# Attention heads taken in pairs whose products alternate between halves of the tensor engine

## The chip, the cores and the metric

The kernel runs on one core of a Trainium2 chip. The metric is the device time of one execution in microseconds, the median of several runs. TensorE (PE in the views, with PEld for its weight loads) does the matrix products, VectorE (DVE) and ScalarE (ACT) the elementwise work, GpSimd (POOL) a little of it, and SyncE (SP) issues the DMAs.

## The reference, cut to what matters

Two decoder layers on 256 tokens of width 1024, in float32. The change lies in the token mixer, which has three branches: a state-space branch (SSM) and two attentions of 8 heads of 64 features. Both attentions of a layer are, for each head,

```
s = q k^T (+ c_q - c_k for the forgetting attention)     # 256 x 256, causal
p = softmax(s)
y = p v                                                   # 256 x 64
```

where `c` is the cumulative log forget gate of the head. The SSM needs `B u` for 512 states at a time, for 256 tokens. Each layer then has a cross-attention and a feed-forward part (dense in layer 0, 8 experts in layer 1).

## The kernel before

The large products are the main work: weights stream in from HBM, ScalarE makes the short-mantissa part of each tile of [128, 1024] (L222, `split`), VectorE the rest (L229), and TensorE multiplies in three single passes (L244 to L246). One unit of main work is one such tile: 12 matmuls of 512 columns (`gemm_xs`) or 24 of 256 columns (`gemm_ws`). After each unit `tick` lets the side generators take a step: `ssm_steps` and `heads` write their instructions between the units. The order on each engine is the one in which the program stands, as a scheduler of the language then leaves it. TensorE runs in that order.

`heads` is called twice in a layer: for the forgetting attention (tiles `fqk`, `forget=True`) beside the projections of the dilated attention, and for the dilated attention (tiles `dqk`) beside the gates and the branch products. It takes one head at a step, in three stages: `weights(h)` (scores into bank `sc`, L860, softmax on VectorE and ScalarE, L868 to L875), two steps later `turn` (three transposes of `p` into bank `pt`, L882, copied by ScalarE to `pts`, L884), one step later `values` (two products into bank `py`, L894 and L896).

A product of float32 operands runs as two instructions (the views show x2 for one product of L860); the main work's float32r products are one each. The tile shape of a product says which part of the 128 x 128 array it uses: main work and transposes 128*128; scores 64*128, since a head has 64 features, and heads 0 and 1 of a pair lie on the lower and the upper 64 rows; values 128*64, the two heads of a pair on the lower and the upper 64 columns; the forget products (L863) 32*128, as the factors `fq` and `fk` have 32 rows (four blocks of eight heads; `fqh` is `fq` with the other heads' rows at zero, made by GpSimd, L856); the SSM input products (`bu`, L729) 64*128; the SSM outputs (L714) 128*32.

The products' banks come from two rotating pools, three in `mm` for the main work and five in `aux` for `sc`, `pt`, `py`, `bu` and others. `p`, `pts` and `fqh` share a pool of eight buffers.

Of the kernel before, what the change touches and what calls it, by code (L numbers as in the profile page):

```python
# [51 lines left out]
class Trunk:  # L52
    """The decoder trunk on one core.

    Products of float32 matrices run as three single-pass products of parts: each operand is
    split exactly into a part with a short mantissa and the rest (float32r tiles)."""
# [46 lines left out]
    # ---------------------------------------------------------------- pools and constants  # L103
# [37 lines left out]
    # ---------------------------------------------------------------- weight stream  # L141
# [197 lines left out]
    # ---------------------------------------------------------------- constants  # L339
    def make_constants(self):  # L340
        nc, c = self.nc, self.const
        # Columns: queries 0-127 against keys 0-127, then queries 128-255 against keys 0-255.
# [7 lines left out]
        # tri[t, q] = 1 where t <= q  # L350
# [8 lines left out]
        # Rows of the forget bias's factors, in blocks of eight heads: one column per block, the last minus  # L359
        # the first.  # L360
# [7 lines left out]
        # For the left and the right factor: weights of the two parts of c, and a constant.  # L368
# [5 lines left out]
        # fmask[p, h] = 1 where p % 8 == h  # L374
        fi = c.tile([32, 2, 8], I32, name="fi")
        nc.gpsimd.iota(fi[:, 0], pattern=[[-1, 8]], base=16, channel_multiplier=1)
        nc.vector.tensor_single_scalar(fi[:, 1], fi[:, 0], 7, op=ALU.bitwise_and)
        self.fmask = c.tile([32, 8], F32, name="fmask")
# [9 lines left out]
        # Channels of even and odd groups of 16.  # L388
# [6 lines left out]
        # The first and the second 64 partitions.  # L395
# [5 lines left out]
        # Keys that the three dilated patterns share count once for each: log of the count.  # L401
# [16 lines left out]
    def sincos(self, ang, sin, cosm1, w):  # L418
        """sin and cos - 1 of ang (which is overwritten), by halved angles; w: a tile as large."""
# [73 lines left out]
    def statistics(self, src):  # L493
        """[mean, 1 / standard deviation] of the tokens of src (two halves of 512 columns)."""
# [56 lines left out]
        # exp(a) - 1: by tanh where |a| < 1.  # L551
# [14 lines left out]
        # lambda_bar - 1 and its quotient by lambda.  # L566
# [17 lines left out]
        # lambda_bar; its square's radius and phase.  # L584
# [8 lines left out]
    def double_angle(self, dst, ph):  # L593
        """dst: (cos, sin) of twice the angle of ph."""
# [7 lines left out]
    def complex_mul(self, dst, src, p, w, conj=False):  # L602
        """dst = src * p (or its conjugate). dst, src: [128, 2, a, b]; p: [128, 2, a]; w: [128, 2, 1024]."""
# [27 lines left out]
        # b_bar and lambda_bar b_bar, in blocks of two groups, transposed to [(lag, 32 channels), 128 states]  # L631
        # for two pieces at a time.
# [19 lines left out]
        # C and minus its imaginary part in the same blocks; then times the conjugate of lambda_bar.  # L652
# [25 lines left out]
        # exp(i 2 theta c) for c < 128 by doubling.  # L678
# [20 lines left out]
    def ssm_steps(self, l):  # L699
        """The states' recurrence as a real one in a turning frame, 512 states at a time; leaves y before  # L700
        the GELU in uy[:, 1], then its GELU."""
# [19 lines left out]
        for k in range(4):  # L721
# [3 lines left out]
            for q in range(4):  # L725
                r = slice(64 * (q % 2), 64 * (q % 2) + 64)
                bu = self.bank(self.aux, "bu")[:, :2 * P].rearrange("p (j c) -> p j c", j=2)
                for j in range(2):
                    nc.tensor.matmul(bu[:, j], bt[r, j, 2 * k + q // 2], us[r, q // 2, k], start=True, stop=True,  # L729
                                     tile_position=(r.start, 0))  # L730
                nc.vector.tensor_mul(v[:, 0, :, q], bu, cc[:, :, q])
                nc.vector.tensor_mul(v[:, 1, :, q], bu, ss[:, :, q])
                if q == 1:
# [23 lines left out]
        # Twice the GELU of y, and the parts of the GELU.  # L757
# [15 lines left out]
    def few_weights(self, src):  # L773
        """Parts of a [1024, 8] matrix, its columns over and over to fill the tensor engine's."""
# [9 lines left out]
    def few_outputs(self, wp):  # L784
        """x @ w for a matrix of 8 columns, as [8, tokens]."""
# [7 lines left out]
    def forget_bias(self, l):  # L793
        """Factors of c_q - c_k over all heads, c the cumulative log forget gates: rows of parts."""
# [12 lines left out]
        # log sigmoid(z) = min(z, 0) - log1p(exp(-|z|))  # L807
# [24 lines left out]
        fq = self.sm([32, S], "fq", bufs=1)  # L832
        fk = self.sm([32, S], "fk", F32R, bufs=1)
        for i, dst in ((0, fq), (3, fk)):
# [4 lines left out]
        self.forget = (fq, fk)  # L839
        yield  # L840

    def heads(self, qk, v, yt, bias, forget=False):
        """Softmax attention of 8 heads, in three stages, two steps and one step apart. qk: [128 (2 heads x 64), 2, 4, 256],
        v: [128 tokens, 2, 512], yt: parts [128, 2, 4, 256] of the transposed result."""
        nc = self.nc
        spans = ((0, slice(0, P)), (1, slice(P, 384)))
        st, py = {}, {}

        def weights(h):
            hp, j = h // 2, h % 2  # L850
            r = slice(64 * j, 64 * j + 64)
            q, k = qk[r, 0, hp], qk[r, 1, hp]
            ps = self.bank(self.aux, "sc")
# [10 lines left out]
            p = self.work([P, 512], "p")  # L864
            mx = self.sm([P, 6], "mx", bufs=4)
            # Minus the scores and minus their maximum.
            for t, cs in spans:
                nc.vector.tensor_tensor_reduce(p[:, cs], ps[:, cs], bias[:, cs], -1.0, 3e38, op0=ALU.add,  # L868
# [586 lines left out]
```

## Time and profile before

| | |
|---|---|
| median of 3 runs (lowest, highest) | 1417.94 us (1417.54, 1419.36) |
| profiled execution: span from its first to its last instruction | 1416.7 us |
| TensorE matmuls busy | 1387.9 us (98%) |
| VectorE busy | 1078.7 us (76%) |
| ScalarE busy | 814.2 us (57%) |
| GpSimd busy | 58.0 us (4%) |

The profiled execution has its span as its own time; the runs' median is 1.2 us above it. Matmuls overlap in the records: one of 512 columns is shown with 0.39 us, and the next starts 0.23 us after it. So a busy share of TensorE hides short stops, and what an instruction costs is read from the distance of the starts. The first product of a new tile shape is recorded from the start of its weight load.

In layer 0 the forgetting attention lies at 100.4 to 157.8 us and the dilated one at 164.0 to 217.5 us; in layer 1 they lie at 678.3 to 737.6 us and 743.9 to 797.6 us.

### The profile page before, as it was taken

Reading aid. Unit: us, or ns where it says so; the run is one execution under the profiler, and the core shown is the slowest. Engines: PE = TensorE matmul, PEld = TensorE weight load, DVE = VectorE, ACT = ScalarE, POOL = GpSimd, SP = SyncE. Lnnn points to the kernel's source line nnn. Section 1 sums busy time; section 2 is a strip of 40 time slices with the busy share of each in tenths; the row PEclk is TensorE's granted clock in tenths of the full one; section 3 lists DMA queues with packets and bytes.
Section 4 is the critical chain, followed back from the end, with each engine's and each line's share of the span. In section 5 each row is a group of like instructions: output and inputs, shape, how many; then the busy total and the mean of one; then the engine's idle time right before and its main releaser. Section 6 shows DMA issues by size and latency. Waiting matters only on the chain. (4 is left out here: it accounts for less than half of the span.)

```text
span 1416.7 us, 22446 instructions
## 1 busy us (share of the span) xinstructions
PE 1387.9 (98%) x8918; PEld 1224.6 (86%) x8918; DVE 1078.7 (76%) x1721; ACT 814.2 (57%) x1170; POOL 58.0 (4%) x79
## 2 busy tenths in 40 slices
PE   7999999999999999999999999998999999999996
PEld 6996889989899999889678999897888888888884
DVE  6797768678585687567666666867899888989887
ACT  4656554445444544434556545443687777877774
POOL 1111000000000000010100000004000000000000
PEclk9999999999999999999999999998999999999998
DMA  9451327755764346635333756563599999999980
GB/s 313 106 179 60 115 88 234 249 179 179 260 191 130 112 129 235 226 118 166 102 100 114 247 183 219 180 253 112 220 364 330 348 349 327 354 346 324 358 326 32
DMA packets 187409, 299.48 MB, mean 211 GB/s; under 512 B 19288, under 2 KB 113568, under 8 KB 187296
## 3 DMA queue, kind: packets, MB, share of 16 engines
q1 hardware_dynamic: 187296, 297.97, 61.4%
q8 instruction: 72, 1.18, 0.3%
q14 instruction: 41, 0.34, 0.1%
HBM read 295.85 MB, written 1.05 MB: 210 GB/s over the span
## 5 line engine op out<-in xcount | busy, mean ns | idle before, releaser
L229 DVE TENSOR_TENSOR split<-raw,split 128x1024 fp32r<-128x1024 f32 (+1 forms) x555 | 648.9, 1191 | 195.8 <-ACT split L222 188.8
L222 ACT CAST split<-raw 128x1024 fp32r<-128x1024 f32 (+1 forms) x558 | 563.8, 1026 | 296.8 <-PE bank L246 96.6
L244 PE MATMUL bank<-xth,split 128*128 128x256 f32 x1056 | 302.2, 286 | 0.0
L245 PE MATMUL bank<-xtl,split 128*128 128x256 f32 x1056 | 298.9, 283 | 0.0
L246 PE MATMUL bank<-xth,split 128*128 128x256 f32 x1056 | 298.8, 283 | 0.0
L244 PEld LDWEIGHTS bank<-xth,split 128*128 128x128 f32 x1056 | 202.3, 192 | 5.9 <-issue 5.1
L245 PEld LDWEIGHTS bank<-xtl,split 128*128 128x128 f32 x1056 | 202.4, 192 | 0.4
L246 PEld LDWEIGHTS bank<-xth,split 128*128 128x128 f32 x1056 | 202.4, 192 | 0.3 <-issue 0.2
L244 PE MATMUL gu<-split,xgh 128*128 128x512 f32 (+1 forms) x384 | 144.4, 376 | 0.0
L245 PE MATMUL gu<-split,xgh 128*128 128x512 f32 (+1 forms) x384 | 143.0, 372 | 0.1
L246 PE MATMUL gu<-split,xgl 128*128 128x512 f32 (+1 forms) x384 | 142.8, 372 | 0.0
L245 PEld LDWEIGHTS gu<-split,xgh 128*128 128x128 f32 x384 | 72.2, 188 | 11.3 <-DVE split L229 1.4
L246 PEld LDWEIGHTS gu<-split,xgl 128*128 128x128 f32 x384 | 72.1, 188 | 10.2
L244 PEld LDWEIGHTS gu<-split,xgh 128*128 128x128 f32 x384 | 72.2, 188 | 10.0
L245 PE MATMUL yd<-split,hth 128*128 128x512 f32 x176 | 69.1, 393 | 0.0
L246 PE MATMUL yd<-split,htl 128*128 128x512 f32 x176 | 68.8, 391 | 0.0
L244 PE MATMUL yd<-split,hth 128*128 128x512 f32 x176 | 62.3, 392 | 0.0
L244 PE MATMUL bank<-split,xth 128*128 128x512 f32 x128 | 54.2, 423 | 5.1 <-ACT xth L234 5.1
L246 PE MATMUL bank<-split,xtl 128*128 128x512 f32 x128 | 51.7, 405 | 0.3 <-DVE xtl L237 0.3
L245 PE MATMUL bank<-split,xth 128*128 128x512 f32 x128 | 51.7, 405 | 0.0
L503 POOL TENSOR_TENSOR lnrs<-lnrs,neghalf 128x1 f32<-128x1 f32 x12 | 11.1, 922 | 976.7 <-DVE lnrs L502 976.7
L871 ACT ACTIVATE p<-p,mx 128x128 f32<-128x128 f32 x64 | 28.7, 449 | 27.0 <-DVE mx L868 26.9
(418 smaller groups left out, 2476.9 us busy)
## 6 DMA issues: line engine op xcount, KB each, us to landing
raw<-in_w_in_dram SPq DMA_DIRECT2D x52, 1024.0 KB, 5.3
raw<-in_moe_w_down_dram SPq DMA_DIRECT2D x40, 1024.0 KB, 6.7
raw<-in_moe_w_gate_dram SPq DMA_DIRECT2D x32, 1024.0 KB, 7.3
raw<-in_moe_w_up_dram SPq DMA_DIRECT2D x32, 1024.0 KB, 7.3
raw<-in_w_branch_dram SPq DMA_DIRECT2D x12, 1024.0 KB, 5.2
raw<-in_moe_w_gate_dram SPq DMA_DIRECT2D x16, 768.0 KB, 7.1
raw<-in_moe_w_up_dram SPq DMA_DIRECT2D x16, 768.0 KB, 6.2
raw<-in_ffn_w_gate_dram SPq DMA_DIRECT2D x11, 1024.0 KB, 5.2
```

The costliest lines, as they stand in the source:

```text
L222: self.nc.scalar.copy(t[:, 0], raw)
L229: self.nc.vector.tensor_sub(t[:, 1], raw, t[:, 0].bitcast(F32))
L244: mm(ps, lh, rh, start=first, stop=False)
L245: mm(ps, lh, rl, start=False, stop=False)
L246: mm(ps, ll, rh, start=False, stop=last)
L503: nc.gpsimd.tensor_tensor(rs[:, 1:2], rs[:, 0:1], self.neghalf, op=ALU.pow)
L871: nc.scalar.activation(p[:, cs], p[:, cs], AF.Exp, bias=mx[:, t:t + 1], scale=-1.0, accum_out=mx[:, 2 + t:3 + t])
```

## The change

Heads are taken in pairs. `weights(hp)` writes the scores of both heads, alternating between the row halves, into two banks, then the forget products of both, then both softmaxes; it runs at even steps. `values(hp)` writes the products of both heads, alternating between the column halves, at even steps, one step after the transposes of the pair's second head. `turn` stays one head at a step. The forget factors become tiles of 128 rows, filled with zeros once at the start, of which the first 32 are written; the masked factor `fqh` of 128 rows is made by ScalarE, no longer by GpSimd, and the forget products use the whole array. In `ssm_steps` two groups of input products take their banks together, and their products alternate between the row halves. Comments were also removed, which moves line numbers: L860, L863, L882 and L894/L896 become L864, L868, L890 and L899, L729 becomes L734.

```diff
 make_constants:
+        self.fq = c.tile([P, S], F32, name="fq")
+        self.fk = c.tile([P, S], F32R, name="fk")
+        nc.gpsimd.memset(self.fq, 0.0)
+        nc.gpsimd.memset(self.fk.bitcast(F32), 0.0)
...
 ssm_steps:
-            for q in range(4):
-                r = slice(64 * (q % 2), 64 * (q % 2) + 64)
-                bu = self.bank(self.aux, "bu")[:, :2 * P].rearrange("p (j c) -> p j c", j=2)
+            for i in range(2):
+                bus = [self.bank(self.aux, "bu")[:, :2 * P].rearrange("p (j c) -> p j c", j=2) for _ in range(2)]
                 for j in range(2):
-                    nc.tensor.matmul(bu[:, j], bt[r, j, 2 * k + q // 2], us[r, q // 2, k], start=True, stop=True,
-                                     tile_position=(r.start, 0))
+                    for bu, r in zip(bus, (slice(0, 64), slice(64, P))):
+                        nc.tensor.matmul(bu[:, j], bt[r, j, 2 * k + i], us[r, i, k], start=True, stop=True,
+                                         tile_position=(r.start, 0))
...
 heads:
-        def weights(h):
...
-            if forget:
-                fq = self.work([32, S], "fqh", F32R)
-                nc.gpsimd.tensor_scalar(fq, self.forget[0], self.fmask[:, h:h + 1], None, op0=ALU.mult)
-            for t, cs in spans:
-                ts = slice(t * P, t * P + P)
-                nk = P * (t + 1)
-                nc.tensor.matmul(ps[:, cs], q[:, ts], k[:, :nk], start=True, stop=not forget,
-                                 tile_position=(r.start, 0))
-                if forget:
-                    nc.tensor.matmul(ps[:, cs], fq[:, ts], self.forget[1][:, :nk], start=False, stop=True)
+        def weights(hp):
+            pair = [self.bank(self.aux, "sc") for _ in range(2)]
+            fqs = []
+            if forget:
+                for j in range(2):
+                    h = 2 * hp + j
+                    fqs.append(self.work([P, S], "fqh", F32R))
+                    nc.scalar.activation(fqs[j], self.fq, AF.Copy, scale=self.fmask[:, h:h + 1])
+            for t, cs in spans:
+                for ps, r in zip(pair, halves):
+                    nc.tensor.matmul(ps[:, cs], qk[r, 0, hp, t * P:t * P + P], qk[r, 1, hp, :P * (t + 1)],
+                                     start=t == 0 or not forget, stop=not forget, tile_position=(r.start, 0))
+            for ps, fq in zip(pair, fqs):
+                for t, cs in spans:
+                    nc.tensor.matmul(ps[:, cs], fq[:, t * P:t * P + P], self.fk[:, :P * (t + 1)],
+                                     start=False, stop=t == 1)
+            for j, ps in enumerate(pair):
...
-        def values(h, pts):
...
+        def values(hp):
+            o = self.bank(self.aux, "py")
+            for kt, (q, c) in enumerate(((slice(0, S), slice(0, S)), (slice(P, S), slice(S, 384)))):
+                for j, r in enumerate(halves):
+                    h = 2 * hp + j
+                    nc.tensor.matmul(o[r, q], v[:, kt, h * HD:(h + 1) * HD], st[h][:, c], start=kt == 0,
+                                     stop=kt == 1, tile_position=(0, r.start))
...
         for i in range(NH + 3):
-            if i >= 3:
-                values(i - 3, st.pop(i - 3))
+            if i % 2 == 0:
+                if i >= 4:
+                    values(i // 2 - 2)
+                if i < NH:
+                    weights(i // 2)
             if 2 <= i < NH + 2:
-                st[i - 2] = turn(st[i - 2])
-            if i < NH:
-                st[i] = weights(i)
+                turn(i - 2)
             yield
```

TensorE at a step of the forgetting attention of layer 0, before (main work is L244 to L246, `py` are values, `pt` transposes, `sc` scores and forget products):

```order
L894 MATMUL py<-pts,vv 64x256
L896 MATMUL py<-pts,vv 64x128
L882 MATMUL pt<-ident,p 128x128 x3
L860 MATMUL sc<-fqk 128x128
L245 MATMUL bank<-split,xth 128x512
L246 MATMUL bank<-split,xtl 128x512
L863 MATMUL sc<-fk,fqh 128x128
L860 MATMUL sc<-fqk 128x256
L863 MATMUL sc<-fk,fqh 128x256
```

This is one head; the tile shapes change with nearly every row. TensorE at an even step of the same stage, after:

```order
L734 MATMUL bu<-us,ssmb 128x128 x4
L899 MATMUL py<-pts,vv 64x256 x2
L899 MATMUL py<-pts,vv 64x128 x2
L864 MATMUL sc<-fqk 128x128 x2
L864 MATMUL sc<-fqk 128x256 x2
L868 MATMUL sc<-fk,fqh 128x128
L868 MATMUL sc<-fk,fqh 128x256
L890 MATMUL pt<-ident,p 128x128 x3
```

These are two heads; the forget products (a 128x128 and a 128x256 for each head) and the transposes have the shape of the main work, and the odd step has the transposes of one head alone. TensorE in the dilated attention of layer 0, one head before:

```order
L894 MATMUL py<-pts,vv 64x256
L896 MATMUL py<-pts,vv 64x128
L882 MATMUL pt<-ident,p 128x128 x3
L860 MATMUL sc<-dqk 128x128
L860 MATMUL sc<-dqk 128x256
L244 MATMUL bank<-xth,split 128x256
```

The same for two heads after:

```order
L899 MATMUL py<-pts,vv 64x256 x2
L899 MATMUL py<-pts,vv 64x128 x2
L864 MATMUL sc<-dqk 128x128 x2
L864 MATMUL sc<-dqk 128x256 x2
L890 MATMUL pt<-ident,p 128x128 x3
L244 MATMUL bank<-xth,split 128x256
```

The scores moved ahead of the transposes, next to the values. ScalarE in the forgetting attention of layer 0, after (`p,mx` are the exponentials, `ytf` the result of a pair; before, no `fqh` stood here):

```order
L892 COPY pts<-pt 128x384
L861 ACTIVATE fqh<-fq,fmask 128x256 x2
L222 CAST split<-raw 128x1024
L901 CAST ytf<-py 128x256
L878 ACTIVATE p,mx<-p,mx 128x128
```

The two `fqh` of the next pair stand behind the copy of the odd head's transposes and ahead of the next split.

## Rows read from the trace of the kernel before

**Rows 1.** The page: span, and each engine's busy time, share and instructions.
```profile
span 1416.7 us, 22446 instructions
PE 1387.9 (98%) x8918; PEld 1224.6 (86%) x8918; DVE 1078.7 (76%) x1721; ACT 814.2 (57%) x1170; POOL 58.0 (4%) x79
```

**Rows 2.** Busy time by stretch: start:end, length, engines, clock, DMA share, GB/s.
```profile
100.40:157.80 57.40, 57.40 (x267) 39.26 (x267) 40.64 (x103) 35.58 (x81) 5.39 (x5) 1.00 0.28 91
...
164.00:217.50 53.50, 53.50 (x441) 45.43 (x438) 40.86 (x100) 31.15 (x74) 0.00 (x0) 1.00 0.37 120
...
678.30:737.60 59.30, 59.30 (x308) 40.97 (x307) 39.83 (x105) 35.88 (x81) 4.58 (x5) 1.00 0.27 89
...
164.00:177.00 13.00, 13.00 (x125) 11.38 (x122) 12.66 (x35) 8.68 (x22) 0.00 (x0) 1.00 0.47 147
```

**Rows 3.** TensorE's waits, largest first: us in total, times, longest.
```profile
PE bank L244 <- ACT xth L234: 5.1, 2, 4.7
```

**Rows 4.** Timeline of TensorE, forgetting attention, one head: start, us, instructions.
```profile
99.83 0.39 PE L245 MATMUL bank<-split,xth 128*128 128x512 f32 x1
100.06 0.39 PE L246 MATMUL bank<-split,xtl 128*128 128x512 f32 x1
100.37 0.49 PE L860 MATMUL sc<-fqk 64*128 64x128 f32 x2
100.79 0.32 PE L863 MATMUL sc<-fk,fqh 32*128 32x128 f32 x1
101.04 0.70 PE L860 MATMUL sc<-fqk 64*128 64x256 f32 x2
101.67 0.38 PE L863 MATMUL sc<-fk,fqh 32*128 32x256 f32 x1
101.98 0.50 PE L244 MATMUL bank<-split,xth 128*128 128x512 f32 x1
102.31 0.40 PE L245 MATMUL bank<-split,xth 128*128 128x512 f32 x1
```

**Rows 5.** Timeline of TensorE, dilated attention, scores of one head.
```profile
167.55 0.28 PE L245 MATMUL bank<-xtl,split 128*128 128x256 f32 x1
167.67 0.28 PE L246 MATMUL bank<-xth,split 128*128 128x256 f32 x1
167.88 0.92 PE L860 MATMUL sc<-dqk 64*128 64x128 f32 x4
168.73 0.38 PE L244 MATMUL bank<-xth,split 128*128 128x256 f32 x1
168.96 0.28 PE L245 MATMUL bank<-xtl,split 128*128 128x256 f32 x1
```

**Rows 6.** Timeline of TensorE, values of one head.
```profile
157.06 0.28 PE L245 MATMUL bank<-xtl,split 128*128 128x256 f32 x1
157.27 0.65 PE L894 MATMUL py<-pts,vv 128*64 128x256 f32 x2
157.75 0.38 PE L896 MATMUL py<-pts,vv 128*64 128x128 f32 x2
158.06 0.39 PE L246 MATMUL bank<-xth,split 128*128 128x256 f32 x1
158.29 0.28 PE L244 MATMUL bank<-xth,split 128*128 128x256 f32 x1
```

**Rows 7.** Timeline of TensorE, products of the SSM on several tiles.
```profile
120.63 0.72 PE L729 MATMUL bu<-us,ssmb 64*128 64x128 f32 x8
121.28 0.65 PE L894 MATMUL py<-pts,vv 128*64 128x256 f32 x2
...
172.02 1.08 PE L714 MATMUL ssmy<-ssmw,ssmct 128*32 128x127 f32 x32
```

**Rows 8.** ScalarE's groups, 100.4 to 157.8 us: busy, mean ns, idle before them.
```profile
L871 ACT ACTIVATE p<-p,mx 128x256 f32<-128x256 f32 x8 | 4.0, 498 | 0.0
...
L871 ACT ACTIVATE p<-p,mx 128x128 f32<-128x128 f32 x8 | 3.2, 403 | 9.8 <-DVE mx L868 9.8
```

More of the change, by code (lines that the diff above doesn't have):

```diff
@@ L373, in make_constants @@
         nc.vector.tensor_add(fw[:, 5:6], fs[:, 2:3], fs[:, 3:4])
-        fi = c.tile([32, 2, 8], I32, name="fi")
+        self.fq = c.tile([P, S], F32, name="fq")
+        self.fk = c.tile([P, S], F32R, name="fk")
+        nc.gpsimd.memset(self.fq, 0.0)
+        nc.gpsimd.memset(self.fk.bitcast(F32), 0.0)
+        fi = c.tile([P, 2, 8], I32, name="fi")
         nc.gpsimd.iota(fi[:, 0], pattern=[[-1, 8]], base=16, channel_multiplier=1)
         nc.vector.tensor_single_scalar(fi[:, 1], fi[:, 0], 7, op=ALU.bitwise_and)
-        self.fmask = c.tile([32, 8], F32, name="fmask")
+        self.fmask = c.tile([P, 8], F32, name="fmask")
         nc.vector.tensor_copy(self.fmask, fi[:, 1])
@@ L724, in ssm_steps @@
             cc, ss = (e[:, j:j + 1].to_broadcast([P, 2, 4, P]) for j in range(2))
[L725 to L727 removed]
+            for i in range(2):
+                bus = [self.bank(self.aux, "bu")[:, :2 * P].rearrange("p (j c) -> p j c", j=2) for _ in range(2)]
                 for j in range(2):
[L729 to L733 removed]
+                    for bu, r in zip(bus, (slice(0, 64), slice(64, P))):
+                        nc.tensor.matmul(bu[:, j], bt[r, j, 2 * k + i], us[r, i, k], start=True, stop=True,
+                                         tile_position=(r.start, 0))
+                for q, bu in enumerate(bus, 2 * i):
+                    nc.vector.tensor_mul(v[:, 0, :, q], bu, cc[:, :, q])
+                    nc.vector.tensor_mul(v[:, 1, :, q], bu, ss[:, :, q])
+                if i == 0:
                     yield
@@ L831, in forget_bias @@
         nc.vector.tensor_sub(cl, pc, ch.bitcast(F32))
-        fq = self.sm([32, S], "fq", bufs=1)
-        fk = self.sm([32, S], "fk", F32R, bufs=1)
-        for i, dst in ((0, fq), (3, fk)):
+        for i, dst in ((0, self.fq[:32]), (3, self.fk[:32])):
             w = self.work([32, S], "fcw")
@@ L838, in forget_bias @@
             nc.vector.scalar_tensor_tensor(dst, cl, self.fwt[:, i + 1:i + 2], w, op0=ALU.mult, op1=ALU.add)
-        self.forget = (fq, fk)
         yield
@@ L846, in heads @@
         spans = ((0, slice(0, P)), (1, slice(P, 384)))
-        st, py = {}, {}
-        def weights(h):
[L850 to L853, printed above, removed]
+        halves = (slice(0, 64), slice(64, P))
+        st = {}
+        def weights(hp):
+            pair = [self.bank(self.aux, "sc") for _ in range(2)]
+            fqs = []
             if forget:
-                fq = self.work([32, S], "fqh", F32R)
-                nc.gpsimd.tensor_scalar(fq, self.forget[0], self.fmask[:, h:h + 1], None, op0=ALU.mult)
+                for j in range(2):
+                    h = 2 * hp + j
+                    fqs.append(self.work([P, S], "fqh", F32R))
+                    nc.scalar.activation(fqs[j], self.fq, AF.Copy, scale=self.fmask[:, h:h + 1])
@@ L870, in weights @@
-            for t, cs in spans:
-                nc.scalar.activation(p[:, cs], p[:, cs], AF.Exp, bias=mx[:, t:t + 1], scale=-1.0,
-                                     accum_out=mx[:, 2 + t:3 + t])
-            nc.vector.reciprocal(mx[:, 4:6], mx[:, 2:4])
-            for t, cs in spans:
-                nc.scalar.mul(p[:, cs], p[:, cs], mx[:, 4 + t:5 + t])
-            return p
-        def turn(p):
+                for ps, r in zip(pair, halves):
+                    nc.tensor.matmul(ps[:, cs], qk[r, 0, hp, t * P:t * P + P], qk[r, 1, hp, :P * (t + 1)],
+                                     start=t == 0 or not forget, stop=not forget, tile_position=(r.start, 0))
@@ new lines, in weights @@
+            for ps, fq in zip(pair, fqs):
[3 more added lines that the diff above has]
+            for j, ps in enumerate(pair):
+                p = self.work([P, 512], "p")
+                mx = self.sm([P, 6], "mx", bufs=4)
+                for t, cs in spans:
+                    nc.vector.tensor_tensor_reduce(p[:, cs], ps[:, cs], bias[:, cs], -1.0, 3e38, op0=ALU.add,
+                                                   op1=ALU.min, accum_out=mx[:, t:t + 1])
+                for t, cs in spans:
+                    nc.scalar.activation(p[:, cs], p[:, cs], AF.Exp, bias=mx[:, t:t + 1], scale=-1.0,
+                                         accum_out=mx[:, 2 + t:3 + t])
+                nc.vector.reciprocal(mx[:, 4:6], mx[:, 2:4])
+                for t, cs in spans:
+                    nc.scalar.mul(p[:, cs], p[:, cs], mx[:, 4 + t:5 + t])
+                st[2 * hp + j] = p
@@ L879, in turn @@
+        def turn(h):
+            p = st[h]
             pt = self.bank(self.aux, "pt")
@@ L882, in turn @@
                 nc.tensor.transpose(pt[:, c * P:(c + 1) * P], p[:, c * P:(c + 1) * P], self.ident)
-            pts = self.work([P, 512], "pts")
-            nc.scalar.copy(pts[:, :384], pt[:, :384])
-            return pts
-        def values(h, pts):
-            hp, j = h // 2, h % 2
-            r = slice(64 * j, 64 * j + 64)
-            if j == 0:
-                py[hp] = self.bank(self.aux, "py")
-            o = py[hp]
-            vs = slice(h * HD, (h + 1) * HD)
-            nc.tensor.matmul(o[r, :S], v[:, 0, vs], pts[:, :S], start=True, stop=False,
-                             tile_position=(0, r.start))
-            nc.tensor.matmul(o[r, P:S], v[:, 1, vs], pts[:, S:384], start=False, stop=True,
-                             tile_position=(0, r.start))
-            if j == 1:
-                nc.scalar.copy(yt[:, 0, hp], o[:, :S])
-                nc.vector.tensor_sub(yt[:, 1, hp], o[:, :S], yt[:, 0, hp].bitcast(F32))
-        for i in range(NH + 3):
-            if i >= 3:
-                values(i - 3, st.pop(i - 3))
+            st[h] = self.work([P, 512], "pts")
+            nc.scalar.copy(st[h][:, :384], pt[:, :384])
+        def values(hp):
[5 more added lines that the diff above has]
+                                     stop=kt == 1, tile_position=(0, r.start))
+            nc.scalar.copy(yt[:, 0, hp], o[:, :S])
+            nc.vector.tensor_sub(yt[:, 1, hp], o[:, :S], yt[:, 0, hp].bitcast(F32))
+        for i in range(NH + 3):
+            if i % 2 == 0:
[3 more added lines that the diff above has]
+                    weights(i // 2)
             if 2 <= i < NH + 2:
-                st[i - 2] = turn(st[i - 2])
-            if i < NH:
-                st[i] = weights(i)
+                turn(i - 2)
             yield
```

4 lines of the change are left out of this document (removed).

## Prediction

> **What bounds the kernel now.** The page first [rows 1]: TensorE has matmuls in flight for 98% of the span, VectorE works 76% of it, ScalarE 57%. That share could hide stops, so I next took the stretches of the attentions [rows 2]: in each TensorE is busy throughout, at the full clock, while VectorE and ScalarE have 57.4 - 40.6 = 16.8 and 21.8 us to spare in the first. The list of TensorE's waits [rows 3] has 5.1 us as its largest entry in the whole span, at a layer's start and not in the attentions. So here the kernel is as fast as TensorE gets through its own list, and what counts is the distance from start to start in it.
>
> There the attentions are dear. A main product of 512 columns takes a slot of 0.23 us (100.06 - 99.83) [rows 4]; one of 256 columns takes 0.12 us [rows 5]. Around one forgetting head the distance from the last whole main slot to the next is 102.31 - 100.06 = 2.25 us; less two main slots, 1.79 us go to this head's scores [rows 4]. In the dilated attention the same without forget products takes 168.96 - 167.67 - 2 x 0.12 = 1.05 us [rows 5], and one head's values take 158.29 - 157.06 - 2 x 0.12 = 0.99 us [rows 6].
>
> **What a change of tile shape costs.** The forgetting head changes shape five times (whole array, 64 rows, 32, 64, 32, whole), the dilated one twice, with the same four score instructions. The difference, 1.79 - 1.05 = 0.74 us, is three changes and the two forget products; these stream 384 columns, which at the main rate (0.23 us for 512) is 0.17 us. A change is then (0.74 - 0.17) / 3 = 0.19 us; with the forget products at nothing it would be 0.25 us, and at twice as much 0.13 us. Four score instructions alone take 1.05 - 2 x 0.19 = 0.67 us. Values are four instructions of the same columns, so 0.99 - 0.67 - 0.19 = 0.13 us is left for the change into 64 columns.
>
> **The change part by part.**
>
> *Fewer changes of shape.* Counted in the program's order, tile shapes change 239 times before and 117 times after; in the four attention stages 63, 36, 65 and 35 become 18, 18, 23 and 18. Of the 122 that go, 108 led into a shape with 128 columns and 14 into 64 columns: 108 x 0.19 + 14 x 0.13 = 22.3 us. With the other two prices of a change it is some 30 or 15 us.
>
> *Halves side by side.* There are 16 pairs of heads (four in each of four stages). If two halves run at once, a pair's scores take one head's 0.67 us, not two. That row halves do is shown by the SSM inputs [rows 7]: eight instructions of 128 columns, four on each half, take 121.28 - 120.63 = 0.65 us with the load before them and the change behind; a score head's two instructions of 128 columns and two of 256 take as many columns as six of these and alone need 0.67 us, so eight in sequence would need 0.89 us and two changes. Less one change, the eight streamed in 0.46 us. For column halves the nearest row is that of quarters: 32 instructions of 127 or 128 columns in 1.08 us [rows 7], where in sequence they would take 3.5 us. No row shows halves of columns; the bounds are nothing and the full gain, and I take the full gain, since four at once run there. Scores: 16 x 0.67 = 10.7 us. Values: at the end of each forgetting stage the order has main products between the two heads, so 14 pairs gain 0.67 and two gain the 128-column third, 0.2: 9.8 us. The price of a change and that of a head's four instructions hang together: at 0.25 us for a change they take 0.55 us, at 0.13 us 0.79 us, so this part and the last together move less than each, from 46 to 39 us.
>
> *Forget products on 128 rows.* After the change four stand in a row per pair; the first follows a change, the others come at the main slot of 0.12 us for 256 columns, which I take for 128 columns too: 0.05 + 3 x 0.12 = 0.41 us against 2 x 0.17: 8 x 0.07 = 0.6 us more.
>
> *SSM inputs.* Nothing: the two halves already ran side by side when all of one half's products stood ahead of the other's [rows 7]. The Trainium skill speaks against this row: "TensorE: Matmul & The Clock Gate", Part 3, says that matmuls start and end strictly in program order and are never reordered. By that rule the eight would have run one after the other until now, and alternating would save 16 x (0.89 - 0.46) = 7 us more; this trace does not agree, as its 0.65 us shows.
>
> *Work that moves to ScalarE.* Sixteen `fqh` leave GpSimd, which no one waits for at its 5.39 us per stage [rows 2], and cost ScalarE 0.50 us each by the exponential of the same shape [rows 8], 4.0 us a forgetting stage. VectorE's work is unchanged; two zero fills on GpSimd at the start are beside idle time.
>
> The sum for TensorE alone: 22.3 + 10.7 + 9.8 - 0.6 = 42.2 us. By stages that is about 13, 9, 13 and 8 us: the first becomes 57.4 - 13.2 = 44.2 us, the second 53.5 - 8.7 = 44.8 us.
>
> **Where a stall would go.** The others' work does not shrink. In the first stage VectorE would be busy 40.6 of 44.2 us (92%) and ScalarE 35.6 + 4.0 = 39.6 (90%); in the second 40.9 of 44.8 (91%) and 31.2 (70%); in layer 1's first 39.8 and 39.9 of 46.7 (85%) [rows 2]. TensorE runs dense beside such an engine in this trace: at 164 to 177 us VectorE is busy 12.66 of 13 us and TensorE 13.00 [rows 2]. But there ScalarE had a third of its time free, and a forgetting pair needs both engines alternately: VectorE's minimum, ScalarE's exponentials, VectorE's reciprocal, ScalarE's scaling, TensorE's transposes, ScalarE's copy, and now the two `fqh` for the next pair behind that copy. TensorE, which runs in order, waits at the forget products if these are late, and all main work is queued behind it. I take 2.5 us for layer 0's forgetting stage, 1.5 for layer 1's, 1 for the dilated ones together: 5 us. From below it is nothing. From above: ScalarE keeps its 9.8 us of idling for VectorE's minimum [rows 8] on top of its 39.6 us, so 49.4 us in place of 44.2, about 5 us in each forgetting stage, and some 3 us in each dilated one: 16 us.
>
> So 1416.7 - 42.2 + 5 = 1379.5 us for the span, and with the 1.2 us by which the runs' median stands above the profiled span, **1381 us**.
>
> **The rivals.**
> - *A: the softmax sets the pace.* With the upper bound of 16 us or a little more, as VectorE's splits are also late, the time is 1385 to 1400 us. For it: two engines at 90% that wait for each other. Against it: the pair's chain has two steps of main work, some 9 us, to run in, and the splits stand buffers ahead. Chance 0.22.
> - *B: column halves do not overlap.* The values keep their 0.67 us a head: 9.8 us less, 1391 us. Against it: the quarters [rows 7]. Chance 0.05.
> - *C: TensorE in strict order*, as that page has it: 7 us more are won at the SSM inputs, 1374 us. Chance 0.02, the 0.65 us being plain.
> - *D: slower than before.* The forget products wait for `fqh`. Each of eight pairs has one such stop; at (42 + 3) / 8 = 5.6 us each the gain is gone, and from there it is slower, say 1422 us. ScalarE would have to be 5.6 us behind in every pair, of 11 us that a pair lasts; it has 1.1 us free in that time and the `fqh` could be made far earlier by the eight buffers, so I give 0.03.
>
> The rest, 0.68, is the forecast, with its own range of 1374 to 1387 us.
>
> **How the numbers follow.** About 0.2%, 2.8 us, is what a measurement of this kernel can tell from no change. The range takes in C and most of A and B: 1373 to 1396 us; outside it are D, the end of A, and a little on the low side. Faster 0.95: the forecast, A, B and C end at least 18 us below 1418. Same 0.02, slower 0.03 from D.
>
> **What would show it.** Right: the score cluster of a dilated pair (eight instructions) followed by a change takes about what one head's four took, and a forgetting pair's scores with forget products about 1.5 us, where two heads took 3.6; the eight value instructions of a pair about 1 us; the SSM cluster still 0.65 us; the four stages near 44, 45, 47 and 45 us, and TensorE's waits in them at most 5 us. Wrong: TensorE waiting for `fqh` or `pts` by more than 10 us in all (A or D), a value pair of 1.6 us (B), or an SSM cluster that was and is different from 0.65 us (C). A stage outside the mixers that changes by more than 1 us would be something that I do not see.

## The result and the profile after

The changed kernel takes 1378.16 us (median of 4 runs, 1377.96 to 1378.54) where the kernel before took 1418.26 us beside it: a ratio of 0.972, 95% interval 0.9708 to 0.9732. The forecast was 1381 us.

The page of the changed kernel, its span and each engine's busy time, against [rows 1]:

```profile
span 1376.6 us, 22435 instructions
...
PE 1346.3 (98%) x8918; PEld 1206.7 (88%) x8918; DVE 1076.5 (78%) x1721; ACT 814.1 (59%) x1186; POOL 38.8 (3%) x65
```

TensorE has as many matmuls as before and is busy 41.6 us less, so what went is time inside its list. For where, I cut each layer's mixer at the first scores of its two attentions and at its end (the last SSM output in layer 0, the last values in layer 1). Windows of the kernel before (start:end, length, engines, clock, DMA share, GB/s):

```profile
100.37:164.07 63.70, 63.70 (x321) 45.00 (x321) 43.65 (x109) 37.44 (x84) 5.39 (x5) 1.00 0.25 82
164.07:248.29 84.22, 84.22 (x741) 74.83 (x737) 66.94 (x141) 45.05 (x91) 0.00 (x0) 1.00 0.50 160
678.31:743.93 65.62, 65.62 (x382) 46.79 (x381) 43.33 (x110) 37.30 (x83) 4.58 (x5) 1.00 0.32 103
743.93:797.70 53.77, 53.77 (x438) 45.66 (x437) 36.83 (x87) 33.84 (x77) 0.00 (x0) 1.00 0.37 122
```

The same four of the changed kernel:

```profile
98.77:150.55 51.78, 51.48 (x321) 40.61 (x322) 42.20 (x109) 38.20 (x90) 0.00 (x0) 1.00 0.32 101
150.55:227.52 76.97, 75.91 (x741) 70.72 (x737) 66.51 (x141) 43.34 (x91) 0.00 (x0) 1.00 0.55 175
657.59:711.76 54.17, 53.95 (x381) 42.14 (x380) 43.19 (x110) 37.79 (x89) 0.00 (x0) 1.00 0.40 121
711.76:757.32 45.56, 45.56 (x438) 41.55 (x437) 35.95 (x87) 32.08 (x77) 0.00 (x0) 1.00 0.44 140
```

The reader is to see four falls, 11.9, 7.25, 11.45 and 8.2 us, 38.8 us in all (267.3 to 228.5); that the matmul counts did not change (x321, x741, x382 to 381, x438); and that the clock is 1.00 in all eight, so none of this is the clock. VectorE's and ScalarE's own times stay within 2 us of what they were, in shorter windows. Between the mixers the two traces agree within 0.1 us; after them the changed kernel is 0.3 us slower. The rest of the 40.1 us is the start-up: the first scores stand at 98.77 in place of 100.37 us. That point lies anywhere from 98.1 to 100.6 us in the twelve profiles of this study, whatever the kernel. The stretch behind the mixers differs too. Near the router of layer 1's experts, where TensorE has a wait of 3.3 us, the granted clock then is 0.5 (1.2 GHz) for some 14 us in five of the profiles and 17 us in seven; from the end of the mixers on, the five take 618.9 to 619.3 us and the seven 619.4 to 620.4. So differences of 1 us between kernels are read below from the mixers ("the four windows"), not from the total.

The stages of the prediction end earlier than these windows. From its first scores to the main product behind its last values, each takes 44.81, 46.49, 47.18 and 45.49 us, where the prediction looked for 44, 45, 47 and 45. The first of them:

```profile
98.77:143.58 44.81, 44.51 (x260) 34.02 (x259) 38.28 (x103) 36.34 (x87) 0.00 (x0) 1.00 0.36 116
```

TensorE's waits in the changed kernel (us in total, times, longest), the largest of the span and the two that lie in the attentions:

```profile
PE bank L244 <- ACT xth L234: 4.6, 2, 4.2
...
PE pt L890 <- DVE ssmw L738: 1.1, 1, 1.1
...
PE py L899 <- ACT pts L892: 0.5, 2, 0.3
```

Timeline of the changed kernel (start, us, instructions): a forgetting pair, the place of the first wait with ScalarE's rows, a dilated pair, the place of the second wait.

```profile
98.45 0.39 PE L246 MATMUL bank<-split,xtl 128*128 128x512 f32 x1
98.77 0.93 PE L864 MATMUL sc<-fqk 64*128 64x128 f32 x8
99.63 0.73 PE L868 MATMUL sc<-fk,fqh 128*128 128x128 f32 x4
100.20 0.39 PE L244 MATMUL bank<-split,xth 128*128 128x512 f32 x1
...
112.18 1.03 ACT L222 CAST split<-raw 128x1024 fp32r<-128x1024 f32 x1
...
113.11 1.49 ACT L882 ACTIVATE p<-p,mx 128x128 f32<-128x128 f32 x4
...
113.43 0.71 PE L734 MATMUL bu<-us,ssmb 64*128 64x128 f32 x8
...
114.07 0.65 PE L899 MATMUL py<-pts,vv 128*64 128x256 f32 x2
...
114.51 0.46 ACT L892 COPY pts<-pt 128x384 f32<-128x384 f32 x1
...
115.02 0.86 PE L899 MATMUL py<-pts,vv 128*64 128x256 f32 x6 [0.30 <-ACT pts L892]
...
165.87 0.87 PE L899 MATMUL py<-pts,vv 128*64 128x256 f32 x8
166.67 0.93 PE L864 MATMUL sc<-dqk 64*128 64x128 f32 x8
167.53 0.55 PE L890 MATMUL pt<-ident,p 128*128 128x128 f32 x3
...
175.51 0.93 PE L864 MATMUL sc<-dqk 64*128 64x128 f32 x8
...
177.50 0.30 PE L890 MATMUL pt<-ident,p 128*128 128x128 f32 x1 [1.06 <-DVE ssmw L738]
```

Against [rows 4], a forgetting pair's scores and forget products take 100.20 - 98.45 - 0.23 = 1.52 us, where two heads took 3.6. Against [rows 5, 6], a dilated pair's eight score instructions take 0.86 us to the next start (167.53 - 166.67), and eight value instructions 0.80 us (166.67 - 165.87). Against [rows 7], the SSM cluster still takes 0.64 us (114.07 - 113.43).

The wait at 114 us: ScalarE has the next pair's softmax to do first. Behind a split it comes to that pair's four scalings (L882) at 113.11, and only behind these, at 114.51, to the copy of the transposes of this pair's second head, while TensorE is at this pair's values from 114.07. The value cluster takes 115.81 - 114.07 = 1.74 us where others take 0.80: 0.94 us lost. The same happens at 683 us (1.66 us, 0.86 lost). At 175.51 scores to transposes take 1.99 in place of 0.86 us, as the transposes wait for a bank that VectorE's SSM products hold: 1.13 us lost. That is 2.9 us in all; the recorded waits show 1.6 us of it, since the records of earlier matmuls run on into the stop (0.39 us is shown for a slot of 0.23).

### The profile page after: what moved, and what is told of

The parts are those of the page before. It is cut to its first block, busy times and chain, and to the rows that moved or that the text cites. A ratio compares the mean times of both kernels' runs of the same rounds, so it can differ in the third digit from the quotient of the medians.

```text
span 1376.6 us, 22435 instructions
## 1 busy us (share of the span) xinstructions
PE 1346.3 (98%) x8918; PEld 1206.7 (88%) x8918; DVE 1076.5 (78%) x1721; ACT 814.1 (59%) x1186; POOL 38.8 (3%) x65
## 5 line engine op out<-in xcount | busy, mean ns | idle before, releaser
L244 PE MATMUL bank<-xth,split 128*128 128x256 f32 x1056 | 302.0, 286 | 0.0
L246 PE MATMUL bank<-xth,split 128*128 128x256 f32 x1056 | 298.7, 283 | 0.0
L244 PEld LDWEIGHTS bank<-xth,split 128*128 128x128 f32 x1056 | 202.3, 192 | 3.5 <-issue 2.7
L246 PEld LDWEIGHTS bank<-xth,split 128*128 128x128 f32 x1056 | 202.4, 192 | 0.1
L244 PE MATMUL gu<-split,xgh 128*128 128x512 f32 (+1 forms) x384 | 144.4, 376 | 0.0
L246 PE MATMUL gu<-split,xgl 128*128 128x512 f32 (+1 forms) x384 | 142.7, 372 | 0.0
L246 PEld LDWEIGHTS gu<-split,xgl 128*128 128x128 f32 x384 | 72.1, 188 | 10.2
L244 PEld LDWEIGHTS gu<-split,xgh 128*128 128x128 f32 x384 | 72.2, 188 | 10.0
L246 PE MATMUL yd<-split,htl 128*128 128x512 f32 x176 | 68.8, 391 | 0.0
L244 PE MATMUL yd<-split,hth 128*128 128x512 f32 x176 | 62.3, 392 | 0.0
L244 PE MATMUL bank<-split,xth 128*128 128x512 f32 x128 | 52.8, 413 | 4.6 <-ACT xth L234 4.6
L246 PE MATMUL bank<-split,xtl 128*128 128x512 f32 x128 | 50.7, 397 | 0.3 <-DVE xtl L237 0.3
```

Of the source, the lines that this page charges most:

```text
L244: mm(ps, lh, rh, start=first, stop=False)
L246: mm(ps, ll, rh, start=False, stop=last)
```

## Experiments

Theory: TensorE is the bound; some half of the gain is tile shapes that change less often (0.19 us each), the other half is two heads side by side in the array. Rivals: halves ran apart before for their written order; the halves give nothing; the softmax or the place where `fqh` is made sets the pace.

**SSM inputs alone.** The kernel before, with the alternation in `ssm_steps` only.

```diff
-            for q in range(4):
-                r = slice(64 * (q % 2), 64 * (q % 2) + 64)
...
+            for i in range(2):
...
+                for j in range(2):
+                    for bu, r in zip(bus, (slice(0, 64), slice(64, P))):
...
```

> The kernel before with the SSM input products alone alternating between the row halves; nothing else is changed. The theory (matmuls on two row halves already run side by side when all of one half's products stand ahead of the other's): no change, within 1 us of 1418 us, and a cluster of eight input products still takes 0.65 us to the next start. The rival (TensorE takes its products strictly in the written order, and alternating is what lets halves overlap): 16 clusters x 0.43 us = 7 us less, 1411 us, and a cluster that falls from about 0.9 to 0.46 us plus the change of shape.

Measured: 1417.84 us, ratio to before 0.9997 (0.9988 to 1.0007); the four windows 267.2 us where before has 267.3. Its timeline:

```profile
118.32 0.72 PE L729 MATMUL bu<-us,ssmb 64*128 64x128 f32 x8
118.97 0.65 PE L895 MATMUL py<-pts,vv 128*64 128x256 f32 x2
```

0.65 us, as in [rows 7]. This part of the change does nothing. The trace of the kernel before shows why: the eight start in four pairs there too. Cut to this cluster, its windows have two instructions under way by 120.70 us, four by 120.90 and six by 121.00:

```profile
120.63:120.70 0.07, 0.07 (x2) 0.07 (x2) 0.00 (x0) 1.00 0.00 0
120.63:120.90 0.27, 0.27 (x4) 0.27 (x6) 0.00 (x0) 1.00 0.11 30
```

With one half alone (the run after the next) they start one by one, 0.11 us and more apart. So the products of the upper half, written behind all four of the lower, do not start behind them, and inside such a cluster TensorE does not keep to the written order. The Trainium skill, "TensorE: Matmul & The Clock Gate", Part 3, has matmuls start and end strictly in the order of the program. By that the alternation would have been worth 7 us, as the prediction estimates it, and neither the run nor the trace agrees.

**Fewer changes of shape, no heads side by side.** The kernel before, one head at a time, with 128-row factors from ScalarE and the forget products behind the scores.

```diff
...
-                fq = self.work([32, S], "fqh", F32R)
-                nc.gpsimd.tensor_scalar(fq, self.forget[0], self.fmask[:, h:h + 1], None, op0=ALU.mult)
+                fq = self.work([P, S], "fqh", F32R)
+                nc.scalar.activation(fq, self.fq, AF.Copy, scale=self.fmask[:, h:h + 1])
...
-                if forget:
-                    nc.tensor.matmul(ps[:, cs], fq[:, ts], self.forget[1][:, :nk], start=False, stop=True)
+            if forget:
+                for t, cs in spans:
+                    nc.tensor.matmul(ps[:, cs], fq[:, t * P:t * P + P], self.fk[:, :P * (t + 1)],
+                                     start=False, stop=t == 1)
```

> The kernel before, one head at a time, with only the forget factors of 128 rows (made by ScalarE) and a head's two forget products behind its two scores. Tile shapes change 60 times less in TensorE's order, and no two heads run side by side. The theory (a change of shape costs 0.19 us and TensorE is the bound): 60 x 0.19 - 0.6 = 10.8 us less, 1407.5 us, nearly all of it in the two forgetting stages; with the price at its bounds of 0.13 and 0.25 us it would be 1411 and 1404 us. The rival that only halves side by side give time, or that what counts is when the softmax gets its data: 1417 to 1420 us. The rival that ScalarE's new work of 4 us a forgetting stage holds the heads up: above 1418 us.

Measured: 1406.69 us, ratio 0.9916 (0.99 to 0.9933). Its four windows:

```profile
100.57:158.78 58.21, 58.21 (x322) 43.76 (x321) 43.19 (x109) 39.55 (x91) 0.00 (x0) 1.00 0.29 90
158.78:243.00 84.22, 84.22 (x741) 74.83 (x737) 67.20 (x141) 44.84 (x91) 0.00 (x0) 1.00 0.51 160
673.07:733.20 60.13, 60.13 (x382) 45.45 (x381) 43.02 (x110) 39.49 (x90) 0.00 (x0) 1.00 0.37 113
733.20:786.97 53.77, 53.77 (x438) 45.66 (x437) 36.86 (x87) 33.85 (x77) 0.00 (x0) 1.00 0.38 122
```

The forgetting windows fall by 5.5 us each and the dilated ones not at all (84.22 and 53.77 twice), a control in the same run. With the 0.6 us that the wider forget products were to cost, (11.0 + 0.6) / 60 = 0.19 us for a change. The Trainium skill, "TensorEngine Tiling (Array Packing)", Key Properties, says that changing the tiling mode drains TensorE. The run agrees in that fewer changes save time, 0.19 us each; that a drain is what takes it no run here shows. ScalarE's added 4 us held nothing up. The run has the gathering of the forget products and their padding to 128 rows together, and does not show what each is worth.

**Scores on one row half.**

```diff
-                for ps, r in zip(pair, halves):
+                for ps, r in zip(pair, (halves[0], halves[0])):
```

> The changed kernel with both heads' scores of a pair taken from the lower row half (so the second head's scores are computed from the first head's queries and keys); instructions, shapes, banks and order are the same. The theory (two halves side by side are worth one head's four instructions, 0.67 us, in each of 16 pairs): 10.7 us more than the changed kernel, 1389 us, if no stall shrinks in exchange; 1387 to 1389 us. The rival that the gain of the pairs is the saved changes of shape alone: 1378 us. The rival that the softmax sets the pace in the forgetting stages, where 4 us of stalls would take in the longer scores: about 1384 us, all of it in the dilated stages.

Measured: 1386.54 us, ratio to before 0.9773 (0.9757 to 0.9789); the four windows 236.0 us, 7.5 more than the changed kernel's. Its timeline at the same dilated pair:

```profile
169.94 1.57 PE L864 MATMUL sc<-dqk 64*128 64x128 f32 x8
171.45 0.55 PE L890 MATMUL pt<-ident,p 128*128 128x128 f32 x3
```

The cluster takes 1.50 us where it took 0.86: halves side by side are worth 0.64 us a pair, 16 x 0.64 = 10.2 us. That only 7.5 us came out, which put the total just under the 1387 to 1389 us expected, is a matter of the waits: the three of the changed kernel, 2.9 us, are gone here (10.2 - 2.9 = 7.3). With more to do between them, TensorE arrives when copy and bank are ready.

**Values on one column half.**

```diff
...
-                for j, r in enumerate(halves):
+            for j, r in enumerate((halves[0], halves[0])):
...
-            nc.scalar.copy(yt[:, 0, hp], o[:, :S])
+            nc.scalar.copy(yt[:64, 0, hp], o[:64, :S])
...
```

> The changed kernel with both heads' values of a pair written to the lower column half, one head behind the other (the second head's result takes the place of the first's, and the upper half of the result is zeros); ScalarE and VectorE read 64 partitions in place of 128, as many columns. Shapes change as often as in the changed kernel. The theory (column halves run side by side, worth 0.67 us a pair): 16 x 0.67 = 10.7 us more, 1387 to 1389 us. The rival that column halves do not overlap and the values' gain came from fewer changes of shape: 1378 us.

Measured: 1388.05 us (four runs, 1386.76 to 1392.62), ratio to before 0.9796 (0.9777 to 0.9815); the four windows of the profiled execution, one of 1386.94 us, take 236.7 us, 8.2 more. Its timeline:

```profile
168.19 1.51 PE L900 MATMUL py<-pts,vv 128*64 128x256 f32 x8
169.64 0.93 PE L865 MATMUL sc<-dqk 64*128 64x128 f32 x8
```

1.44 us in place of 0.80, again 0.64 us a pair: column halves run side by side, which no row of before showed. Fourteen pairs at 0.64 and two that are split by main work at 0.21 make 9.4 us. Two of the three waits are gone and the third shrinks to 0.3 us, 2.6 us less; 1.4 us of new stops make up the rest, 0.9 of them where the transposes of the dilated queries wait for VectorE's rotations.

**`fqh` back on GpSimd.**

```diff
-                    nc.scalar.activation(fqs[j], self.fq, AF.Copy, scale=self.fmask[:, h:h + 1])
+                    nc.gpsimd.tensor_scalar(fqs[j], self.fq, self.fmask[:, h:h + 1], None, op0=ALU.mult)
```

> The changed kernel with the masked forget factors made by GpSimd again, as before the change (128 rows now). The theory (TensorE's own list is the bound, and ScalarE has the time for its 4 us of forget factors in a forgetting stage): no change, 1377 to 1379 us; the two late copies of transposed heads, for which TensorE waits 0.9 us each, stay, since the factors stand behind those copies. The rival that ScalarE's added work makes the copies late: both waits go, 1376.4 us. The rival that leaving GpSimd was itself a gain (1.08 us for each factor there, forget products waiting for it): 1380 us or more.

Measured: 1378.36 us, ratio to before 0.9724 (0.9711 to 0.9737); the four windows 228.3 us (changed kernel: 228.5). The engine doesn't matter for the time, as expected, but not for the reason given. Of the two late copies the first now comes in time (its value cluster takes 0.81 us), and the second costs 0.65 us in place of 0.86. What the first gains is lost a little later: the transposes behind the next forget products wait for a bank that VectorE's SSM products hold. TensorE's timeline there:

```profile
115.28 0.72 PE L868 MATMUL sc<-fk,fqh 128*128 128x128 f32 x4
116.59 0.52 PE L890 MATMUL pt<-ident,p 128*128 128x128 f32 x3 [0.59 <-DVE ssmw L738]
```

From the forget products to the transposes it is 1.31 us in place of 0.57, 0.74 us lost. The four forget products themselves take what they take elsewhere (0.72 and 0.73 us), so GpSimd's factors are in time. Their durations (ns: least, median, most):

```profile
L861 POOL TENSOR_SCALAR fqh<-fq,fmask x16: 917/926/3281, 63.2 to 678.3; 128x256 fp32r<-128x256 f32 x16
```

**Scores ahead of values.**

```diff
+                if i < NH:
+                    weights(i // 2)
                 if i >= 4:
                     values(i // 2 - 2)
-                if i < NH:
-                    weights(i // 2)
```

> The changed kernel with the scores and forget products of a pair written ahead of the values of the pair before, which gives ScalarE 1.4 us more to copy the transposed head. Shapes change once more in all. The theory (the changed kernel loses 0.9 us at each of two late copies, and the rest of TensorE's time is its list): both waits go, 1.8 - 0.2 = 1.6 us less, 1376.6 us. The rival that the pair's chain of softmax is as long as the time between its steps: the wait moves to the transposes, and the time is 1378 us or more.

Measured: 1379.3 us, ratio to before 0.9726 (0.9712 to 0.9739). The four windows take 227.7 us, 0.75 less than the changed kernel's, where 1.6 was expected. The two late copies are no longer waited for, and the dilated window of layer 0 is 1.3 us shorter (75.67 us), but the first is 1.2 us longer (52.96): the forget products now wait for `fqh`, which stands behind the same late copy on ScalarE, and the rotated queries are waited for. Its waits in layer 0's mixer:

```profile
PE sc L868 <- ACT fqh L861: 0.6, 1, 0.6
PE dqt L935 <- DVE dq L926: 0.5, 1, 0.5
```

So in the first stage the rival was right that the wait moves, though it went to the forget products and the rotated queries, not to the transposes. The total, too, is in the rival's range, but part of that is the late start-up of this profile (100.57 us).

**SSM inputs of a piece in one cluster.**

```diff
...
-                bus = [self.bank(self.aux, "bu")[:, :2 * P].rearrange("p (j c) -> p j c", j=2) for _ in range(2)]
+            bus = [self.bank(self.aux, "bu").rearrange("p (i j c) -> p i j c", i=2, j=2) for _ in range(2)]
...
```

> The changed kernel with the SSM input products of a piece in one cluster of 16 instructions rather than two of eight, in two banks rather than four. Shapes change 11 times less in TensorE's order. The theory: 11 x 0.19 = 2.1 us less, and a wait of 1.1 us for a bank that VectorE's SSM products hold in the dilated stage may go too: 1375 to 1376 us. The rival that the longer hold of the banks makes transposes or scores wait: 1378 us or more.

Measured: 1379.57 us, ratio to before 0.9726 (0.9712 to 0.9739). Layer 1 gained: its windows take 52.17 and 45.37 us, 2.2 us less; 0.4 of that come back ahead of them, where a cluster of SSM inputs now stands, and of the 1.8 that stay 0.8 are the late copy, no longer waited for. Layer 0 lost 2.9 us, 2.8 of them in its first window, by a new wait, as the rival had it, and by what followed. Windows of that place, and TensorE's timeline there:

```profile
118.00:120.30 2.30, 0.48 (x3) 0.08 (x2) 2.30 (x9) 0.00 (x0) 0.00 (x0) 1.00 0.31 33
120.30:123.70 3.40, 3.40 (x10) 2.82 (x11) 3.18 (x16) 3.11 (x12) 0.00 (x0) 0.51 0.84 286
123.70:130.00 6.30, 6.30 (x40) 4.61 (x40) 6.07 (x14) 5.27 (x10) 0.00 (x0) 1.00 0.01 3
```

```profile
118.01 0.40 PE L245 MATMUL bank<-split,xth 128*128 128x512 f32 x1
120.22 0.83 PE L891 MATMUL pt<-ident,p 128*128 128x128 f32 x3 [1.82 <-DVE ytf L903]
120.70 0.78 PE L246 MATMUL bank<-split,xtl 128*128 128x512 f32 x1
121.28 0.63 PE L244 MATMUL bank<-split,xth 128*128 128x512 f32 x1
121.70 0.63 PE L245 MATMUL bank<-split,xth 128*128 128x512 f32 x1
```

Of the five banks two are now held until the next step by the SSM products, two by scores and one by values, so the transposes wait until VectorE has read the values, behind four SSM products: 2.0 us. Then the granted clock is 0.51 for 3.4 us and a main product takes 0.43 us (121.70 - 121.28) in place of 0.23. The wait cost about as much again after it was over: some 1.7 us, half of the 3.4. This fall of the clock seems not to come each time, since the two shortest of the five executions (1376.23 and 1377.93 us) have a mean granted clock of 0.991 and the other three (1379.57 to 1381.1 us, the profiled one among them) of 0.989.

**Both edits**, the last two diffs together.

> The changed kernel with both edits, scores ahead of values and SSM input products in one cluster. Shapes change 9 times less. The theory: 9 x 0.19 = 1.7 us for the changes of shape and 1.8 to 2.9 us for the waits, 1373.6 to 1374.7 us. The rival that VectorE and ScalarE, each at some 85% in the forgetting stages, now set the time: 1376 us or more, with more waits of TensorE than in the changed kernel.

Measured: 1380.64 us, ratio to before 0.9741 (0.9728 to 0.9755), the four windows 229.5 us. The expectation failed in the same place, and the rival's time, 1376 us or more with more waits, came out: TensorE's transposes wait 3.6 us in layer 0 for banks that VectorE has yet to read, and the clock is 0.68 from 121 to 124 us. Layer 1 gained as with the single cluster alone.

**What paid, stage by stage.** Scores first only in the dilated attention, the single cluster only in layer 1.

```diff
...
+                if i < NH and not forget:
+                    weights(i // 2)
                 if i >= 4:
                     values(i // 2 - 2)
-                if i < NH:
+                if i < NH and forget:
...
+            if l == 1:
+                bus = [self.bank(self.aux, "bu").rearrange("p (i j c) -> p i j c", i=2, j=2) for _ in range(2)]
...
```

> The changed kernel with what paid, stage by stage, in the two runs before: scores ahead of values in the dilated attentions alone, and the SSM input products of a piece in one cluster of 16 in layer 1 alone. The theory (the stages add up, since each is TensorE's list plus its own waits): the mixer of layer 0 takes 127.4 us from its first scores to its last SSM output, that of layer 1 97.5 us, 3.5 us less than the changed kernel in all, 1374.7 us, give or take 1.5 us for the start-up. The rival that a wait moved out of one stage comes back in the next: the two mixers take 228 us or more, as in the changed kernel.

> The changed kernel as it is, for a comparison beside the run with the mixed edits: 1378 us, and the two mixers 128.7 and 99.7 us; only the start-up ahead of the first attention may differ, by 1 to 2 us, as it does between all profiles so far.

Measured: the mixed kernel 1375.43 us (1374.76 to 1375.86), ratio to before 0.9704 (0.9691 to 0.9717); the changed kernel beside it 1378.04 us, 0.9726 (0.9712 to 0.9739), with mixers of 128.7 and 99.7 us. The mixed kernel's windows:

```profile
98.62:150.38 51.76, 51.48 (x322) 40.62 (x323) 42.16 (x109) 38.06 (x90) 0.00 (x0) 1.00 0.32 101
150.38:226.04 75.66, 75.66 (x741) 70.63 (x737) 66.36 (x141) 43.17 (x91) 0.00 (x0) 1.00 0.57 178
656.50:708.72 52.22, 52.22 (x373) 41.79 (x372) 42.42 (x110) 37.90 (x89) 0.00 (x0) 1.00 0.39 123
708.72:754.08 45.36, 45.36 (x438) 41.48 (x437) 36.07 (x87) 32.02 (x77) 0.00 (x0) 1.00 0.45 143
```

127.4 and 97.6 us, as expected: the stages add up, and the windows are 3.4 us shorter than those of the changed kernel beside it. Of that 0.4 come back between the mixers, as in the run with the single cluster, and 0.3 after them. The two start-ups agree here (98.62 and 98.63 us), and the medians differ by 2.6 us. The ratios' intervals overlap a little, but each of the five executions of the mixed kernel is shorter than each of the changed kernel's (at most 1375.86, at least 1377.19 us), and the windows show where the gain is.

## Why the prediction was right

- *The bound.* TensorE's own list: with the same number of matmuls, time fell only where the list was cheaper. The run with padded factors alone shows it best: its dilated windows, with the list unchanged, keep their time to 0.01 us.
- *A change of shape*, forecast at 0.19 us from one head's rows, came to 0.19 us over 60 changes. The 0.13 us into 64 columns has no run of its own.
- *Halves side by side.* A head's four instructions were put at 0.67 us and are 0.64: scores 10.2 us in place of 10.7, values 9.4 in place of 9.8. The step without a row of its own, that column halves overlap as quarters do, held.
- *Forget products.* Four in a row with the change ahead of them take 0.57 us (100.20 - 99.63), forecast 0.60, so 0.3 us more in all in place of 0.6.
- *SSM inputs.* Nothing, in the changed kernel and alone.
- *The sum for TensorE alone* was 42.2 us. The windows' 38.8 and the 2.9 us of waits make 41.7; less scores, values and forget products (10.2 + 9.4 - 0.3) the changes of shape are left with 22.4 us, forecast 22.3. That is a remainder and not a measurement: 60 of the 122 changes were run by themselves.
- *Stalls*, the mis-sized term: 5 us forecast, 2.9 found, as 0.94 in layer 0's forgetting stage (2.5 forecast), 0.86 in layer 1's (1.5) and 1.13 in the dilated ones (1). Where they would lie was half right: values waited for the copy of `pts`, and transposes for a bank that SSM products held, which the prediction had not named; nowhere did the forget products wait for `fqh`. The forecast took the others' work into the shorter stage whole, and there was less of it: VectorE was busy 38.28 of the first stage's 44.81 us (85%, forecast 92%) and ScalarE 36.34 (81%, forecast 90%). That this is why the stalls are fewer was not run.
- *The total.* 1381 forecast, 1378.16 measured. Of the 2.9 us by which the profiled span lies below the forecast span, 1.6 are the start-up, which nothing in the change accounts for: that part is luck. The waits, 2.1 us shorter than forecast, less the smaller terms (0.5) and the 0.3 us behind the mixers make the rest.

The rivals: A (softmax sets the pace) did not come true, though two engines at 81 and 74% in the first window leave little: each of the other orders tried (scores first, one SSM cluster, both) made layer 0's first window longer, by a wait in another place. B and C fell by the run for each. D fell: factors made by GpSimd, slower still (median 0.93 us, ScalarE 0.50), were not waited for. Its mechanism showed only where the scores stood ahead of the values, at most 0.6 us at a time.

## What to carry to other kernels

Where TensorE never waits, read what a product costs from the distances of starts, and count how often the tile shape changes: small products of one shape are worth gathering, and padding a contraction to the full array, so that it has the shape of its neighbours, can be part of that. Products on the two row halves overlap without being alternated in the program, as the SSM's eight show; what counted there is that they stood together. For column halves only the alternating order was run. An experiment that adds work to the bounding engine shows that work less the waits it fills, so read the cluster's own length beside the total; and an edit that holds a bank longer has to be tried stage by stage, as its new wait can cost more than the changes of shape that it saves.

## What the hardware showed unexpectedly

- After the 2.0 us stop at 118 us with the single SSM cluster, TensorE was granted 0.51 of its clock (1.2 GHz) for 3.4 us, though it had been dense before and was dense again. The run with both edits has the same: a stop of 2.0 us at 119 us, and half the clock for 3.4 us from 122 us. Stops of 1.7 and 1.9 us near 182 us in these two runs, and of 0.9 to 1.1 us in the changed kernel, were followed by the full clock. Why the ones fell and the others not was not tried.
- The masked factor takes GpSimd as long for 128 rows as for 32: the median of sixteen is 0.93 and 0.92 us. Single ones take up to 3.3 and 2.8 us; the 5.39 us for five of [rows 2] hold one of 1.74.
- The start-up ahead of the first attention differs by up to 2.5 us between profiles, also of kernels that are alike there, as much as several of the edits tried here.
